# Prompt's mean squares inside the sample's projection, its norm buffers laid out first, v by head group, halo queries copied on DVE

## The chip, the cores and the metric

The kernel runs on one core of one Trainium2 chip. The metric is the device time in microseconds (us) of one execution; the time of a kernel is the median of several. The engines of a core work beside one another, each on its own instruction list in order: TensorE (PE, with its weight load PEld), VectorE (DVE), ScalarE (ACT), GpSimd (POOL) and SyncE (SP). SP and ACT also issue DMAs, each on a queue of its own; both queues end in the core's 16 DMA engines.

## The reference

One layer of a transformer trunk is applied to two sequences that share all weights: the prompt (1024 tokens) and the sample (512 tokens), each with 16 meta tokens in front, so 1040 and 528 rows of 1024 features, all in float32.

```
n    = rms_norm(x, g_mix);  proj = n @ w_in                      # 18 blocks of 128 columns
qa, ka, va (group A: 8 query heads, 2 key/value heads)           # q and k: rms_norm per head, then rope
oa   = softmax(qa ka^T * scale) va
qb, kb, vb (group B: 4 heads, each with two maps)                # rope
ob   = (softmax(q0 k0^T) - lambda * softmax(q1 k1^T)) vb;  rms_norm(ob)
x    = x + concat(oa, ob) @ w_out
n    = rms_norm(x, g_ffn)
gate = conv3(n @ w_gate) + b                                     # 3 taps along the tokens
x    = x + (gelu(gate) * (n @ w_up)) @ w_down
y    = rms_norm(x, g_final)                                      # without the 16 meta tokens
```

The convolution looks one token to either side, so of the 16 meta tokens only the last one (column 0 of the tensors `oT`) is needed behind the attention. It is got from a small extra block of queries, the halo: two columns, tokens 14 and 15, of each of the four query heads that share a key/value head.

## The kernel before

A product in float32 is made of three `fp32r` matmuls (`mm3`, L129 to L131): each operand is split into a high part (a cast on ACT, L123) and the rest (a subtraction on DVE or POOL, L124). `dense` does 8 such triples for one output tile of 128 rows by a chunk of tokens; the prompt's chunks are 384, 384 and 272 tokens wide, the sample's 256 and 272.

The work goes in five stages: (1) the sample's projection; (2) the sample's attention merged with the prompt's projection; (3) the prompt's attention merged with the sample's output projection and feed-forward part; (4) the prompt's output projection; (5) its feed-forward part. Each part is a Python generator. `merge` draws from two of them in turn by their counted cost; `LEAD1` and `LEAD2` set how far one starts ahead, and the first `HOLD` steps of the later one are held behind a mark. Within that, the framework's scheduler and its pools set the order of each engine's list. The list is then fixed: an instruction that waits holds up everything behind it on its engine. SP issues nearly all loads and stores but the weights (these go through ACT's queue, L146). Its DMAs take eight completion semaphores in turn, and each waits for the one that used the semaphore before it.

The places that the change touches:

- `projection(0)` first reads x, casts it, and adds up the squares on POOL in `acc` (L199). Then come the dense tile of the first chunk of `KA` (the keys of group A), three matmuls of `acc` with a constant matrix (`ones_d`, L208, one for each chunk) and behind each the reciprocal root on ACT and DVE (`rsqrt_newton`, L112 to L117) with `eps2` (L210), which the head norms of q and k need.
- `keys_a` (from L273) then takes each chunk through dense, a square on ACT (`sq`, L286), rope on DVE (L287, L290), `head_norm` (POOL L228, matmul L232, L112 to L117, L240) and the stores of the split result (`finish`, L247).
- Buffers come from pools that are opened and closed like a stack, from the left end of the memory for the prompt and the right for the sample. The pool `pt0` holds `sq`, `hn` and `rs_y`; it is opened behind `pb0`, which holds `y`, `z`, `hi`, `t` and `v`. A pool that is laid over a closed one takes over its waits, tile by tile: the first write to `sq` waits for the last reads of what lay there, among them a store of the sample's `y` (its pool `pb1` ended with the sample's projection).
- `attention` loads q in pairs of tiles of 512 columns (`stacked`, L370), k (L370), v (L389, `v_tail` L391), and for each head and 512 queries does four score blocks (`softmax`: matmuls L401 and L402, eviction on DVE L405 with the minimum, exponential on ACT L408). There is one score tile in PSUM, so each block waits for the eviction of the one before. The halo's queries come by 8 loads of 128 x 2 columns for each key/value head, 16 for each sequence. `reciprocals` sends a row through memory (`rT`, L458) and reads it back spread over partitions (`o_rb`, L474). The outputs go to `oT` (L563 for group B).
- Behind the sample's last head, `mixer_out` loads `h` from `oT` (L615) and residues `res` (memset L631, load L628).

## Time and profile before

| | |
|---|---|
| median of 3 runs | 2257.44 us (2257.15 to 2257.8) |
| profiled execution | 2256.74 us |
| its span | 2254.9 us |
| mean granted TensorE clock | 0.973 |
| PE busy | 2131.7 us (95%) |
| DVE, ACT, POOL busy | 1270.8, 1039.8, 666.4 us |

So 1.84 us of the profiled execution lie outside its span, and it is 0.70 us below the median. PE is busy nearly throughout and idle for 123 us in all. Below, a row of the timeline is: start, duration, engine, line, operation, output from inputs, and in square brackets how long the engine had been idle and what ended that. A row of waits is: engine and what waited, from what it waited for, total us, times, longest. A row of the chain of waits is: start, duration, what. SPq and ACTq are the queues' issuing instructions; a row with xN groups N of them.

### The profile page before, as it was taken

Reading aid. Unit: us, or ns where it says so; the run is one execution under the profiler, and the core shown is the slowest. Engines: PE = TensorE matmul, PEld = TensorE weight load, DVE = VectorE, ACT = ScalarE, POOL = GpSimd, SP = SyncE. Lnnn points to the kernel's source line nnn. Section 1 sums busy time; section 2 is a strip of 40 time slices with the busy share of each in tenths; the row PEclk is TensorE's granted clock in tenths of the full one; section 3 lists DMA queues with packets and bytes.
Section 4 is the critical chain, followed back from the end, with each engine's and each line's share of the span. In section 5 each row is a group of like instructions: output and inputs, shape, how many; then the busy total and the mean of one; then the engine's idle time right before and its main releaser. Section 6 shows DMA issues by size and latency. Waiting matters only on the chain.

```text
span 2254.9 us, 32335 instructions
## 1 busy us (share of the span) xinstructions
PE 2131.7 (95%) x12442; PEld 1912.1 (85%) x12442; DVE 1270.8 (56%) x2203; ACT 1039.8 (46%) x1830; POOL 666.4 (30%) x514
## 2 busy tenths in 40 slices
PE   6887999986799999999999997999999999999997
PEld 6886999985698888888999996998888888888887
DVE  6635554454658667667777775774433444433446
ACT  5434554655647444566777775552112221112224
POOL 5862345531023221234444443431111000111005
PEclk9998999996899999999999998999999999999999
DMA  6573453443332322232333214631111111111112
GB/s 207 177 222 110 145 162 121 158 156 113 118 101 77 94 85 84 67 94 90 115 101 107 88 66 150 191 112 53 47 38 56 47 47 48 47 38 57 47 38 76
DMA packets 114259, 222.76 MB, mean 99 GB/s; under 512 B 16312, under 2 KB 67384, under 8 KB 113592
## 3 DMA queue, kind: packets, MB, share of 16 engines
q1 hardware_dynamic: 85304, 115.82, 16.0%
q10 hardware_dynamic: 28800, 104.87, 14.6%
q8 instruction: 98, 1.61, 0.3%
q14 instruction: 57, 0.47, 0.1%
HBM read 172.10 MB, written 48.55 MB: 98 GB/s over the span
## 4 chain that ended last, share of the span: by engine, by line
PE 82%; DVE 6%; DMA 6%; ACT 3%; issue 2%; POOL 1%; SPq 1%; ACTq 0%; DVEq 0%; POOLq 0%
PE ps_mm L129 20%; PE ps_mm L130 20%; PE ps_mm L131 20%; PE ps_t L422 5%; PE ps_s L401 4%; PE ps_s L402 3%; PE ps_o L437 2%; PE ps_o L436 2%; DMA q<-qk 1%; DMA v<-v 1%; DMA w_f<-w_out 1%; DVE p L405 1%; PE ps_p L129 1%; PE ps_p L131 1%; PE ps_p L130 1%
## 5 line engine op out<-in xcount | busy, mean ns | idle before, releaser
L129 PE MATMUL ps_mm<-xhi,w_hi 128*128 128x512 f32 (+6 forms) x1968 | 663.7, 338 | 0.6 <-ACT w_hi L123 0.6
L130 PE MATMUL ps_mm<-xlo,w_hi 128*128 128x512 f32 (+6 forms) x1968 | 658.3, 335 | 0.0
L131 PE MATMUL ps_mm<-xhi,w_lo 128*128 128x512 f32 (+6 forms) x1968 | 658.2, 335 | 0.0
L129 PEld LDWEIGHTS ps_mm<-xhi,w_hi 128*128 128x128 f32 x1968 | 372.9, 190 | 27.3 <-ACT w_hi L123 0.9
L130 PEld LDWEIGHTS ps_mm<-xlo,w_hi 128*128 128x128 f32 x1968 | 373.1, 190 | 24.9 <-issue 0.5
L131 PEld LDWEIGHTS ps_mm<-xhi,w_lo 128*128 128x128 f32 x1968 | 372.8, 189 | 24.7 <-issue 0.2
L123 ACT CAST w_hi<-w_f 128x1024 fp32r<-128x1024 f32 x134 | 139.3, 1048 | 391.8 <-PE ps_mm L130 353.9
L405 DVE TENSOR_SCALAR_CACHE_REDUCE p<-ps_s 114x1044 f32<-114x1044 f32 (+5 forms) x212 | 223.5, 1054 | 138.9 <-PE ps_s L402 108.2
L124 POOL TENSOR_TENSOR a_lo<-gate,a_hi 128x512 fp32r<-128x512 f32 x66 | 98.8, 1498 | 649.2 <-ACT a_hi L123 648.2
L123 ACT CAST pt_hi<-ps_t 128x512 fp32r<-128x512 f32 (+6 forms) x360 | 169.1, 483 | 204.6 <-PE ps_t L422 174.1
L408 ACT ACTIVATE p<-p,nm 114x1040 f32<-114x1040 f32 (+5 forms) x212 | 215.1, 1015 | 86.2 <-DVE p L405 72.1
L724 DVE TENSOR_TENSOR h<-ps_mm,h 128x512 f32<-128x512 f32 (+1 forms) x288 | 182.4, 645 | 122.2 <-PE ps_mm L131 121.4
L124 DVE TENSOR_TENSOR pt_lo<-ps_t,pt_hi 128x512 fp32r<-128x512 f32 (+4 forms) x312 | 171.7, 564 | 131.9 <-ACT pt_hi L123 129.7
L401 PE MATMUL ps_s<-k,q 128*114 128x348 f32 (+4 forms) x552 | 181.3, 334 | 42.5 <-DMA q<-qk 16.9
L130 PE MATMUL ps_mm<-a_lo,w_hi 128*128 128x512 f32 (+1 forms) x576 | 216.2, 378 | 0.0
L131 PE MATMUL ps_mm<-a_hi,w_lo 128*128 128x512 f32 (+1 forms) x576 | 215.8, 378 | 0.0
L129 PE MATMUL ps_mm<-a_hi,w_hi 128*128 128x512 f32 (+1 forms) x576 | 214.9, 385 | 0.4 <-DVE h L724 0.4
L422 PE MATMUL ps_t<-ident,p 128*128 128x128 f32 (+7 forms) x1188 | 183.7, 270 | 0.4 <-DVE pt_lo L124 0.3
L402 PE MATMUL ps_s<-k,q 128*114 128x348 f32 (+4 forms) x552 | 175.4, 323 | 4.3 <-DMA q<-qk 4.3
L124 DVE TENSOR_TENSOR w_lo<-w_f,w_hi 128x1024 fp32r<-128x1024 f32 x100 | 124.1, 1250 | 83.1 <-ACT w_hi L123 82.9
L422 PEld LDWEIGHTS ps_t<-ident,p 128*128 128x128 f32 (+7 forms) x1188 | 142.7, 136 | 29.2 <-issue 4.5
L532 POOL TENSOR_TENSOR p<-p 114x1040 f32<-114x1040 f32 (+2 forms) x56 | 115.0, 2054 | 128.9 <-ACT p L531 126.9
(193 smaller groups left out, 3530.7 us busy)
## 6 DMA issues: line engine op xcount, KB each, us to landing
w_f<-w_gate ACTq DMA_DIRECT2D x44, 512.0 KB
w_f<-w_up ACTq DMA_DIRECT2D x44, 512.0 KB
w_f<-w_down ACTq DMA_DIRECT2D x44, 512.0 KB
w_f<-w_in ACTq DMA_DIRECT2D x36, 512.0 KB
w_f<-w_out ACTq DMA_DIRECT2D x32, 512.0 KB
q<-qk SPq DMA_DIRECT2D x48, 256.0 KB
q<-qk SPq DMA_DIRECT2D x48, 171.0 KB
qk<-hi SPq DMA_DIRECT2D x20, 384.0 KB
```

The costliest lines, as they stand in the source:

```text
L123: return (nc.scalar.copy(hi, src), (lo_engine or nc.vector).tensor_tensor(out=lo, in0=src, in1=hi.bitcast(F32), op=ALU.subtract))
L124: (lo_engine or nc.vector).tensor_tensor(out=lo, in0=src, in1=hi.bitcast(F32), op=ALU.subtract))
L129: nc.tensor.matmul(ps, lhsT=whi, rhs=xhi, start=start, stop=False)
L130: nc.tensor.matmul(ps, lhsT=whi, rhs=xlo, start=False, stop=False)
L131: return nc.tensor.matmul(ps, lhsT=wlo, rhs=xhi, start=False, stop=stop).ins
L401: nc.tensor.matmul(ps[:, i], lhsT=q[0], rhs=kc, start=True, stop=False)
L402: nc.tensor.matmul(ps[:, i], lhsT=q[1], rhs=kc, start=False, stop=True)
L405: nc.vector.tensor_scalar(out=p.rearrange("p (i w) -> p i w", i=nch), in0=ps, scalar1=-HD ** -0.5, scalar2=3.0e38, op0=ALU.mult, op1=ALU.m ...
L408: nc.scalar.activation(p, p, AF.Exp, bias=nm, scale=-1.0, accum_out=l)
L422: nc.tensor.transpose(tps[:, c:c + M], p[:, k0:k0 + kw], g.ident[:M, :M])
L532: nc.gpsimd.tensor_tensor(out=p0, in0=p0, in1=p1, op=ALU.add)
L724: nc.vector.tensor_tensor(out=hs, in0=ps, in1=hs, op=ALU.add)
```

## The change

Five things change at once, all before the third stage is well under way:

1. The prompt's mean squares leave the handover. The generator `projection(0)` now yields once behind them and before the load of the first weights of `KA`. The main program takes `STATS` = 26 steps of the sample's projection, then this first step of the prompt's, then the rest of the sample's.
2. For the prompt `pt0` is opened ahead of `pb0`, and stays open as long as `pb0` does.
3. `keys_a` of the prompt does the dense tile of the next chunk ahead of the rest of the chunk before, and `LEAD1` goes from -19200 to -20000.
4. v of group A lies in DRAM by key/value head (`[128, 2, tiles, 128]` in place of `[128, tiles, 256]`), so a load of v is one run of 4 KB for each of 128 partitions (before: 8 of 512 B), and its stores are two for each chunk.
5. The q tiles of the first 512 queries are 514 columns wide and start 2 columns earlier; the halo's queries are copied from them by DVE, two copies of 128 x 2 for each head, behind the eviction of the head's second block, in place of the 32 halo loads. The halo's output goes to `oT` in one store for each key/value head, before in four. The small buffers `l_b` and `r_b` have 6 copies, before 8.

```diff
@@ -176,7 +176,8 @@
             out.append(tb)
         return out
 
-    first = load_weight(g, g.w_in[KA])
+    if s == 1:
+        first = load_weight(g, g.w_in[KA])
 
     with tc.tile_pool(name=f"ps{s}", bufs=2, side=side, reuse_waits="tile") as sp:
         if s == 1:
@@ -198,8 +199,9 @@
             elif k:
                 nc.gpsimd.tensor_tensor(out=acc, in0=acc, in1=x, op=ALU.add)
         c0, cw = chunks[0]
-        first_ps = g.psum.tile(P, cw, tag)
-        dense(g, first_ps, first, xhi, xlo, c0, cw)
+        if s == 1:
+            first_ps = g.psum.tile(P, cw, tag)
+            dense(g, first_ps, first, xhi, xlo, c0, cw)
         for i, (c0, cw) in enumerate(chunks):
             if s == 1:
                 ps = ms[i]
@@ -210,9 +212,18 @@
             nc.vector.tensor_scalar(out=eps2[:, c0:c0 + cw], in0=ps, scalar1=EPS, scalar2=2 * EPS,
                                     op0=ALU.add, op1=ALU.mult)
         nc.vector.tensor_scalar(out=rstd, in0=rstd, scalar1=-0.5, scalar2=None, op0=ALU.mult)
+    if s == 0:
+        yield 0
+        first = load_weight(g, g.w_in[KA])
+        c0, cw = chunks[0]
+        first_ps = g.psum.tile(P, cw, tag)
+        dense(g, first_ps, first, xhi, xlo, c0, cw)
     es = ExitStack()
+    if s == 0:
+        tp = pool(ctx, g, f"pt{s}", 2, side)
     bp = pool(ctx, g, f"pb{s}", 2, side)
-    tp = pool(es, g, f"pt{s}", 2, side)
+    if s == 1:
+        tp = pool(es, g, f"pt{s}", 2, side)
     tab = load_tables(0)
     tab_b = load_tables(1) if s == 1 else None
     scales = {KA: [g.gain[:, V_GK:V_GK + 1], g.negain[:, V_GK:V_GK + 1]],
@@ -273,13 +284,9 @@
     def keys_a():
         cos, sin = tab
         gk, ngk = scales[KA]
-        for c0, cw in chunks:
+
+        def rest(ps, c0, cw):
             cc = slice(c0, c0 + cw)
-            if c0 == 0:
-                ps = first_ps
-            else:
-                ps = g.psum.tile(P, cw, tag)
-                dense(g, ps, first, xhi, xlo, c0, cw)
             y = tmp(bp, "y", 1, cw, 3)
             z = tmp(bp, "z", 1, cw, B1)
             sq = tmp(tp, "sq", 1, cw, 1)
@@ -291,7 +298,20 @@
                                                in1=sin[of:of + HD, cc], op0=ALU.mult, op1=ALU.mult)
             nc.gpsimd.tensor_tensor(out=y, in0=y, in1=z, op=ALU.add)
             finish(y, head_norm(sq, g.ones_hd, c0, cw, HD), g.ka[s], True, c0, cw)
+
+        late = []
+        for c0, cw in chunks:
+            if c0 == 0:
+                ps = first_ps
+            else:
+                ps = g.psum.tile(P, cw, tag)
+                dense(g, ps, first, xhi, xlo, c0, cw)
+            late.append((ps, c0, cw))
+            if s == 1 or len(late) == 2:
+                rest(*late.pop(0))
             yield 25 * cw
+        if late:
+            rest(*late.pop())
 
     def values(j):
         w = load_weight(g, g.w_in[j], lo_engine=nc.gpsimd)
@@ -321,7 +341,12 @@
                 split(g, hi, lo, pv)
                 t0 = c0 // P
                 if kw == P:
-                    nc.sync.dma_start(out=dst[:, t0 + i0:t0 + i1, :], in_=v.bitcast(F32)[:, i0:i1, :])
+                    part = v.bitcast(F32)[:, i0:i1, :]
+                    if j == VA:
+                        for m in range(2):
+                            nc.sync.dma_start(out=dst[:, m, t0 + i0:t0 + i1], in_=part[:, :, m * P:(m + 1) * P])
+                    else:
+                        nc.sync.dma_start(out=dst[:, t0 + i0:t0 + i1], in_=part)
                     continue
                 for r, part in ((16, 0), (48, 0)) if j == VA else ((16, 0), (48, 0), (80, 1)):
                     cc = slice(0, 2 * P) if j == VA else slice(part * P, (part + 1) * P)
@@ -372,7 +397,7 @@
     def load_q(j, m, c0, cw):
         out = []
         for first in range(2):
-            q = qp.tile([P, 512], F32R, name="q", tag=f"q{first}")[:, :cw]
+            q = qp.tile([P, 514], F32R, name="q", tag=f"q{first}")[:, :cw]
             stacked(q, j, m, first, c0, cw)
             out.append(q)
         return out
@@ -385,8 +410,8 @@
         return k
 
     def load_v(i, w, c0):
-        v = vp.tile([P, nf, 2 * P], F32R, name="v", tag="v")[:, :, :w]
-        nc.sync.dma_start(out=v.bitcast(F32), in_=g.v[s][i][:, :, c0:c0 + w])
+        v = vp.tile([P, nf * 2 * P], F32R, name="v", tag="v")[:, :nf * w].rearrange("p (t c) -> p t c", c=w)
+        nc.sync.dma_start(out=v.bitcast(F32), in_=g.v[s][0][:, c0 // P] if i == 0 else g.v[s][i])
         tail = vp.tile([P, P], F32R, name="v_tail", tag="v_tail")[:64 if i == 0 else 96]
         nc.sync.dma_start(out=tail.bitcast(F32), in_=g.vt[s][i][:tail.shape[0], c0:c0 + P])
         return v, tail
@@ -402,8 +427,8 @@
             nc.tensor.matmul(ps[:, i], lhsT=q[1], rhs=kc, start=False, stop=True)
 
         nm = sp.tile([P, 1], F32, name="nm", tag="nm")[:M]
-        nc.vector.tensor_scalar(out=p.rearrange("p (i w) -> p i w", i=nch), in0=ps, scalar1=-HD ** -0.5, scalar2=3.0e38,
-                                op0=ALU.mult, op1=ALU.min, accum_out=nm)
+        g.evicted = nc.vector.tensor_scalar(out=p.rearrange("p (i w) -> p i w", i=nch), in0=ps, scalar1=-HD ** -0.5,
+                                            scalar2=3.0e38, op0=ALU.mult, op1=ALU.min, accum_out=nm).ins
         p = p[:, :n]
         nc.scalar.activation(p, p, AF.Exp, bias=nm, scale=-1.0, accum_out=l)
         return p
@@ -485,15 +510,20 @@
     for kv in range(2):
         k = load_k(KA, kv)
         v = load_v(0, P, kv * P)
+        halo = [sp.tile([P, 8], F32R, name="halo", tag=f"halo{f}", bufs=2) for f in range(2)]
         for i in range(4):
             h = kv * 4 + i
             for b in range(nblk):
-                q = load_q(QA + 2 * kv, i, NMETA + 512 * b, 512)
+                q = load_q(QA + 2 * kv, i, NMETA + 512 * b - 2, 514)
                 load_r()
                 pl = []
                 l = sp.tile([P, 4], F32, name="l_a", tag="l_a", bufs=3)
                 for t in range(4):
-                    pl.append(softmax([x[:, t * P:(t + 1) * P] for x in q], k, l[:, t:t + 1]))
+                    pl.append(softmax([x[:, 2 + t * P:2 + (t + 1) * P] for x in q], k, l[:, t:t + 1]))
+                    if t == 1 and b == 0:
+                        with tc.issue_after(g.evicted):
+                            for f in range(2):
+                                nc.vector.tensor_copy(halo[f][:, 2 * i:2 * i + 2], q[f][:, 0:2])
                     yield 2 * n
                 cols = slice(1 + 512 * b, 513 + 512 * b)
                 reciprocals(l, g.rT[s][h, cols].rearrange("(t p) -> t p", p=P))
@@ -501,10 +531,6 @@
                 oa = finish_a(o, W)
                 store_a()
                 late.append((oa, g.rT[s][h:h + 1, cols], g.oT[s][h * HD:(h + 1) * HD, cols]))
-        halo = [sp.tile([P, 8], F32R, name="halo", tag=f"halo{f}", bufs=2) for f in range(2)]
-        for i in range(4):
-            for f in range(2):
-                stacked(halo[f][:, 2 * i:2 * i + 2], QA + 2 * kv, i, f, NMETA - 2, 2)
         l = sp.tile([P, 4], F32, name="l_a", tag="l_a", bufs=3)[:8, 0:1]
         load_r()
         p = softmax(halo, k, l)
@@ -513,17 +539,16 @@
         nc.scalar.activation(p, p, AF.Copy, scale=r)
         o, W = yield from weighted_v([p], v, False)
         oa = finish_a(o, W)
-        for i in range(4):
-            h = kv * 4 + i
-            nc.sync.dma_start(out=g.oT[s][h * HD:(h + 1) * HD, 0:1], in_=oa[:, 2 * i + 1:2 * i + 2])
+        nc.sync.dma_start(out=g.oT[s][kv * 4 * HD:(kv + 1) * 4 * HD, 0:1].rearrange("(i p) o -> p i o", p=HD),
+                          in_=oa.rearrange("p (i o) -> p i o", o=2)[:, :, 1:2])
         store_a()
 
     def diff_block(qs, ks, v, cols):
         pl = []
         for c0, M in cols:
-            l = sp.tile([P, 2], F32, name="l_b", tag="l_b")[:M]
+            l = sp.tile([P, 2], F32, name="l_b", tag="l_b", bufs=6)[:M]
             p0, p1 = [softmax([x[:, c0:c0 + M] for x in qs[m]], ks[m], l[:, m:m + 1]) for m in range(2)]
-            r = sp.tile([P, 2], F32, name="r_b", tag="r_b")[:M]
+            r = sp.tile([P, 2], F32, name="r_b", tag="r_b", bufs=6)[:M]
             nc.vector.reciprocal(out=r, in_=l)
             nc.scalar.activation(p0, p0, AF.Copy, scale=r[:, 0:1])
             c = sp.tile([P, 1], F32, name="c", tag="c")[:M]
@@ -803,7 +828,7 @@
 ML = 2
 NRAW, NW = 2, 3
 R1, R2 = (1.0, 1.1), (1.0, 1.0)
-LEAD1, LEAD2, HOLD = -50 * 384, 60000.0, 4
+LEAD1, LEAD2, HOLD, STATS = -20000.0, 60000.0, 4, 26
 
 
 @with_exitstack
@@ -817,7 +842,8 @@
         n = N + NMETA
         g.qk.append([dram.tile([3, 2, P, n], F32, name=f"qk{s}_{i}") for i in range(len(PAIRS))])
         g.ka.append(dram.tile([2, 2, HD, n], F32, name=f"ka{s}"))
-        g.v.append([dram.tile([P, n // P, 2 * P], F32, name=f"v{s}_{i}") for i in range(5)])
+        g.v.append([dram.tile([P, 2, n // P, P] if i == 0 else [P, n // P, 2 * P], F32, name=f"v{s}_{i}")
+                    for i in range(5)])
 
         g.vt.append(dram.tile([5, 96, 2 * P], F32, name=f"vt{s}"))
         g.oT.append(dram.tile([D, N + 1], F32, name=f"oT{s}"))
@@ -887,11 +913,15 @@
 
     g.psum = Psum(tc, "psa", mm=3)
     g.psum.relay(p=3, t=2)
-    with ExitStack() as es:
-        drain(projection(es, g, 1, "right", "p", "t"))
-    g.psum.relay(s=1, t=2, o=1)
     with ExitStack() as es0:
         p0 = projection(es0, g, 0, "left", "mm", "mm")
+        with ExitStack() as es:
+            p1 = projection(es, g, 1, "right", "p", "t")
+            for _ in range(STATS):
+                next(p1)
+            next(p0)
+            drain(p1)
+        g.psum.relay(s=1, t=2, o=1)
         with ExitStack() as es1:
             merge(g, attention(es1, g, 1, "right"), R1[0], p0, R1[1], LEAD1, HOLD)
         drain(p0)
```

In the lists of the engines, this is PE's at the handover from the first stage to the second. The matmuls with `xhi` and `xlo` are dense ones (`xhi_1674` or `xhi_1309` is the first of the eight), `acc` is the sum of squares, `sq` with `ones_hd` the head norm. Before:

```order
L130 MATMUL ps_mm<-xlo_1689,w_hi 128x384
L131 MATMUL ps_mm<-xhi_1681,w_lo 128x384
L208 MATMUL ps_mm<-acc,ones_d 128x384 x2
L208 MATMUL ps_mm<-acc,ones_d 128x272
L232 MATMUL ps_mm<-sq,ones_hd 128x384
L129 MATMUL ps_mm<-xhi_1674,w_hi 128x384
L130 MATMUL ps_mm<-xlo_1682,w_hi 128x384
```

and now:

```order
L129 MATMUL ps_mm<-xhi_1316,w_hi 128x384
L130 MATMUL ps_mm<-xlo_1324,w_hi 128x384
L131 MATMUL ps_mm<-xhi_1316,w_lo 128x384
L243 MATMUL ps_mm<-sq,ones_hd 128x384
L129 MATMUL ps_mm<-xhi_1309,w_hi 128x272
L130 MATMUL ps_mm<-xlo_1317,w_hi 128x272
L131 MATMUL ps_mm<-xhi_1309,w_lo 128x272
```

The three L208 stand no longer here (they are L210 now, one at row 538 and two at rows 658 and 659, between dense tiles of the sample's projection), the dense tile of the second chunk (rows 929 to 952) is done before the first head norm, and that of the third chunk follows it at once.

Behind these come the sample's first score blocks, each of two pairs of matmuls L401 and L402 (now L426 and L427). Before, two blocks stood behind the second dense tile and three behind the third, each time with a head norm after them, and then the first dense tile of the next weights. Now one block stands behind the third dense tile, then a head norm, three blocks, the third chunk's head norm and the next weights' first dense tile.

This is SP's list where the prompt's attention begins. `qk_0_60`, `qk_1_61` and `qk_2_62` are prompt's q and k in DRAM, `ka_66` its keys of group A, `oT_88` the sample's attention output. Before:

```order
L563 DMA oT_88<-o_b 128x207
L370 DMA q<-qk_0_60 128x1x512
L370 DMA halo<-qk_0_60 128x1x2 x8
L370 DMA k<-ka_66 128x1x1040
L370 DMA k<-ka_66 128x1x4
L389 DMA v<-v_0_67 128x8x128
L391 DMA v_tail<-vt_72 64x128
L370 DMA halo<-qk_1_61 128x1x2 x6
L563 DMA oT_88<-o_b 128x306
L370 DMA halo<-qk_1_61 128x1x2 x2
L370 DMA k<-qk_2_62 128x1x1040
L370 DMA k<-qk_2_62 128x1x4
```

and now:

```order
L395 DMA q<-qk_0_60 128x1x514 x3
L395 DMA k<-ka_66 128x1x1040
L395 DMA k<-ka_66 128x1x4
L414 DMA v<-v_0_67 128x1024
L416 DMA v_tail<-vt_72 64x128
L395 DMA k<-qk_2_62 128x1x1040
L395 DMA k<-qk_2_62 128x1x4
L395 DMA k<-qk_2_62 128x1x1040
L395 DMA k<-qk_2_62 128x1x4
L588 DMA oT_88<-o_b 128x306
L395 DMA q<-qk_0_60 128x1x514
```

The sixteen halo loads are gone, and the v load is one of 128 x 1024; the loads of k and the stores of the sample's last outputs stand directly behind one another. A few rows earlier, three of the prompt's q loads now stand ahead of a sample's q load that they stood behind or beside.

## The prediction

> **What bounds the kernel now.** I read the page first, then the waits of PE, then the chain of waits and the timeline around each long hole.
>
> ```profile
> span 2254.9 us, 32335 instructions
> ...
> PE 2131.7 (95%) x12442; PEld 1912.1 (85%) x12442; DVE 1270.8 (56%) x2203; ACT 1039.8 (46%) x1830; POOL 666.4 (30%) x514
> ...
> PE   6887999986799999999999997999999999999997
> ```
>
> PE is the bound: 123 us idle in 2254.9. A slice is 56.4 us, so the weak digits are slices 1 to 4 (up to 226 us), 9 to 11 (451 to 620) and 25. The rows below say what PE waited for.
>
> ```profile
> PE ps_s L401 <- DMA q<-qk: 16.9, 5, 5.1
> PE ps_s L401 <- DVE p L405: 13.8, 18, 4.0
> PE ps_mm L232 <- POOL sq L228: 12.5, 1, 12.5
> ...
> PE ps_s L401 <- DVE res L631: 11.4, 1, 11.4
> ```
>
> Three places carry it. The 12.5 is one hole at the handover from the sample's projection to its attention (hole 1), the 16.9 lies in the sample's last head (hole 2), the 11.4 at the start of the prompt's attention (hole 3). The chain of waits through hole 1, and ACT's timeline:
>
> ```profile
> 165.31 10.64 DMA qk<-y
> ...
> 176.59 1.00 POOL sq L228
> ```
> ```profile
> 176.02 0.49 ACT L286 ACTIVATE sq<-ps_mm 128x384 f32<-128x384 f32 x1 [9.73 <-DMA qk<-y]
> ```
>
> POOL is only the last link: ACT stood 9.73 us in front of `sq`, whose input had been ready since about 160.4, until a store of the sample's `y` had landed at 175.95, because `sq` lies where that `y` lay.
>
> **Hole 1: the norm buffers and the order of chunks.** PE's rows of the stretch, and the next weights' first dense tile in the chain:
>
> ```profile
> 160.37 1.45 PE L208 MATMUL ps_mm<-acc,ones_d 128*128 128x384 f32 x4
> 164.07 1.10 PE L208 MATMUL ps_mm<-acc,ones_d 128*128 128x272 f32 x2 [2.25 <-DVE eps L210]
> 177.63 1.65 PE L232 MATMUL ps_mm<-sq,ones_hd 128*128 128x384 f32 x2 [12.46 <-POOL sq L228]
> 186.44 0.91 PE L232 MATMUL ps_mm<-sq,ones_hd 128*128 128x384 f32 x2
> 196.41 0.59 PE L401 MATMUL ps_s<-k,q 128*128 128x264 f32 x1 [4.00 <-DVE p L405]
> ```
> ```profile
> 181.50 0.18 PE ps_mm L130
> ...
> 188.98 0.13 PE ps_mm L130
> ...
> 198.57 0.32 PE ps_mm L129
> ```
>
> From 160.37 (first dense tile done) to 198.57 are 38.2 us. With `pt0` laid out first, `sq` waits for PE alone. I walk through the new list with these rows and the following ones of ACT, DVE and POOL:
>
> ```profile
> 179.32 0.49 ACT L112 ACTIVATE rs_y<-ps_mm 128x384 f32<-128x384 f32 x1 [1.50 <-PE ps_mm L232]
> ```
> ```profile
> 181.60 0.56 DVE L115 SCALAR_TENSOR_TENSOR hn<-ps_mm,hn 128x384 f32<-128x384 f32 x1
> ...
> 185.03 0.71 DVE L405 TENSOR_SCALAR_CACHE_REDUCE p<-ps_s 128x528 f32<-128x528 f32 x1 [1.23 <-PE ps_s L402]
> 185.66 0.61 DVE L287 SCALAR_TENSOR_TENSOR y<-ps_mm,gain,rope 128x384 f32<-128x384 f32 x1
> ```
> ```profile
> 160.87 1.34 POOL L124 TENSOR_TENSOR y<-y,hi 128x544 fp32r<-128x544 f32 x1
> ```
>
> - Second dense tile, 24 x 0.18: to 164.6. Beside it ACT's square (0.49) and POOL's addition (1.00, behind the sample's last split, which ends at 162.2): ready at 163.2.
> - Head norm 0.9: 165.5. The third dense tile takes over its PSUM buffer, so it waits for three ACT steps of about 0.5, the second chunk's `sq` between them (0.5) and DVE's L115 (0.56): 2.6 us, 168.1.
> - Third dense tile, 24 x 0.13, and 1.5 for the clock (below): 172.7. First score block, four matmuls of 0.13, and a head norm: 174.1.
> - DVE from 168.1: eight steps of the head norms and rope (0.56 to 0.61) and the eviction (0.73) make 5.5, so the second block starts at 174.1, not later. The third waits for the next reciprocal root (1.6 on ACT, 0.56 on DVE) and the eviction: 177.0. The fourth: 178.5. Behind three more DVE steps that free a PSUM buffer the next dense tile starts at about 180.1.
>
> That is 19.7 us for 38.2, so 18.5 less. One score block of 0.5 is left for later, and the three mean-square matmuls are now paid at full clock among dense tiles, 1.45 + 0.5 (two thirds of a 384's 0.73). **Net -16.0.** Their roots, nineteen ACT and DVE steps of 0.5 to 0.6 or some 10 us, go beside the first stage's dense tiles. For `acc` there is room:
>
> ```profile
> 88.51 2.40 POOL L199 TENSOR_TENSOR acc<-acc,x 128x1040 f32<-128x1040 f32 x1
> ```
>
> Bounds: three q loads were issued ahead of that `y` store, so they had landed by 175.95 at the latest; if the first block gets its two no sooner, it starts 3.3 us later: -12.7. If the clock stays full and the ACT steps lie better: -18.
>
> The clock: at 164.07 the 128x272 pair took 1.10 where 0.52 is its share of the row above, after only 2.25 us of idleness; that is half speed, and I charge the third tile half of its time again. The Trainium skill, "TensorE: Matmul & The Clock Gate", "What's actually happening", has the clock halved after at least one idle window of about 3.4 us. By that a wait of 2.6 us costs no clock and the sum would be 1.5 lower. This trace's row differs, and I go by the row.
>
> **Hole 3: what SP is late with.** PE, then DVE, then SP:
>
> ```profile
> 593.32 0.66 PE L401 MATMUL ps_s<-k,q 128*128 128x348 f32 x1 [11.44 <-DVE res L631]
> ```
> ```profile
> 572.67 0.53 DVE L544 SCALAR_TENSOR_TENSOR o_b<-o_b,gsub,o_rs 128x306 f32<-128x306 f32 x1
> ...
> 579.24 0.68 DVE L124 TENSOR_TENSOR pt_hi<-ps_t,pt_hi 32x512 fp32r<-32x512 f32 x1
> ...
> 592.04 0.06 DVE L631 MEMSET res<- 128x1 f32 x1
> ```
> ```profile
> 534.37 12.21 SPq L370 DMA_DIRECT2D halo<-qk  x8
> ...
> 549.76 8.56 SPq L370 DMA_DIRECT2D halo<-qk  x6
> ...
> 558.89 1.08 SPq L370 DMA_DIRECT2D halo<-qk  x2
> ...
> 572.53 0.46 SPq L458 DMA_DIRECT2D rT<-r_rows  x1
> 580.86 0.49 SPq L474 DMA_DIRECT2D o_rb<-rT  x1
> 581.44 1.13 SPq L370 DMA_DIRECT2D q<-qk  x2
> 582.66 0.43 SPq L563 DMA_DIRECT2D oT<-o_b  x1
> ```
>
> DVE was free at 579.9 and stood until 592.0 in front of a memset of `res`, which takes the place of an `o_b` that still had to be stored. That `o_b` was done at 573.2, but its store was issued at 582.66: behind `o_rb`, which waited 8.3 us for `rT`, which SP reached late, behind 21.85 us of halo loads. It landed 9.4 us after its issue. The list has the same store behind the same `rT`, `o_rb` and q loads, without the halos. SP then reaches `rT` when its row is there (some 564), `o_rb` by 572.5 at most, and the store at about 573.3, when `o_b` is done. With 9.4 us to land: 582.7, a hole of 2.8; with half of that, none. I take **-10** (the store's 9.4 went through queues that two q loads had just filled; without the jam they drain sooner). Bounds 0 (the store waits as before) and -12.9 (the hole, and 1.5 of clock behind it as at hole 1).
>
> **Hole 2: the v load and the sample's last q.**
>
> ```profile
> 504.58 3.40 SPq L389 DMA_DIRECT2D v<-v  x1
> 508.02 6.92 SPq L391 DMA_DIRECT2D v_tail<-vt  x1
> ...
> 515.67 2.95 SPq L370 DMA_DIRECT2D q<-qk  x2
> ```
>
> The prompt's v load, 1024 runs of 512 B, held SP for 10.3 us; as 128 runs it should cost about 1, like the other loads. But the new list puts one prompt q ahead of the sample's next pair and two ahead of the pair after it, and q loads are what those PE waits end with. The bytes are the same and only their order changes, so I take **-1**, with bounds -6 (a third of the 16.9 goes) and +3 (one q load: in the 10.64 of the chain a store landed behind three of them, so some 2.7 each).
>
> **The copies.** Thirty-two DVE copies of 128x2 have no row; the nearest are
>
> ```profile
> 572.01 0.17 DVE L453 RECIPROCAL r_a<-l_a 128x4 f32<-128x4 f32 x1
> ...
> 575.70 0.07 DVE L613 MEMSET h<- 128x8 f32 x1
> ```
>
> so 32 x 0.07 to 0.17 = 2.2 to 5.4 us of DVE. A copy can delay the third block's eviction by 0.2; where dense tiles stand between the blocks PE doesn't notice. I take +1 of 0 to 5.4; without that cover it is all of it. The stores of v in twice as many pieces and the smaller `l_b`, `r_b` come at nothing: SP idles for `rT` alone 8.3 us.
>
> **Sum:** -16 - 10 - 1 + 1 = -26. From the profiled 2256.74 (span and 1.84 around it) 2230.7; its median counterpart stands 0.70 higher: **2231.4**.
>
> **The rivals.**
> - *A, hole 3 stays.* The store still follows two q loads, and `h` and `res` start as late. For: nothing shows `rT`'s 8.3 us to be due to the halos. Against: SP was busy with halos in 21.85 of the 25.6 us from 534.37. -16 - 1 + 1: 2241.4.
> - *B, hole 1 is filled by q loads or by ACT.* ACT now issues weights and a cast between the head norm's steps, and these wait for dense tiles and stores. For: the 4.00 at 196.41 is such a chain. If two thirds of hole 1 come back, -5 for -16: 2242.4.
> - *C, slower.* The first mean-square matmul sits at row 538 of PE's list, by its neighbours some 102 us in; `acc` ended at 90.9. From the point where it ends later than 102, PE stands for each us, and so do the ACT casts behind the root. To eat 26 us and more it must come at 130 or later, because its additions share POOL with the splits; with 132, 2261. Against: PE was full there, and 11 us are spare.
> - *D, it doesn't do what it says.* `pb0` now lies over the sample's buffers: if DVE's first `t` or `v` waits for the same store and that lands later than 184, hole 1 only moves; with hole 3 kept by A only the 2.25 us at 164.07 are won: 2255.2.
>
> **How the numbers follow.** Forecast 0.55, A 0.20, B 0.13, D 0.07, C 0.05. Below, all bounds good: -18 - 12.9 - 6 = -36.9, so 2220; above, A and B together give -4 to -7, so 2250. This leaves out C, D and a little. A measurement tells 0.2%, 4.5 us, from no change: faster 0.87, same 0.08, slower 0.05.
>
> **What would show it.** Right: ACT's `sq` within 1 us of the first dense tile; the next weights' dense tile at 178 to 184; no halo row on SP; the `o_b` store issued by 575 and PE's wait for `res` under 3 us. Wrong: a wait of DVE or ACT for `qk<-y` between 160 and 185; PE waiting for `q<-qk` as long as before plus what the others save; a hole before 110 us at L210.

## The result, and the profile after

| | before | changed |
|---|---|---|
| median of 4 runs each | 2257.30 us (2254.76 to 2257.80) | 2235.88 us (2229.83 to 2236.75) |
| profiled execution, its span | 2256.74, 2254.9 us | 2229.83, 2228.0 us |
| mean granted clock | 0.973 | 0.977 |

The changed kernel takes 0.9902 of the time before (95% interval 0.9882 to 0.9921): 21.4 us less by the medians, where 26 were forecast (2231.4, range 2220 to 2250). A second series gave 2233.04 us and 0.9903. The page of the changed kernel, which is of its fastest execution:

```profile
span 2228.0 us, 32312 instructions
...
PE 2131.8 (96%) x12442; PEld 1912.6 (86%) x12442; DVE 1269.7 (57%) x2235; ACT 1039.7 (47%) x1830; POOL 668.5 (30%) x514
...
PE   7898999986999999999999998999999999999997
```

PE's busy time is the same to 0.1 us, so the difference is idle time: 123.2 us before, 96.2 now. The digits of slices 3 and 4 have gone from 8 and 7 to 9 and 8, and slice 11 (564 to 620 us before) from 7 to 9; slice 10 is still 6. What PE waits for now:

```profile
PE ps_s L426 <- DMA q<-qk: 19.0, 6, 7.2
PE ps_s L426 <- DVE p L430: 12.4, 19, 2.2
...
PE ps_t L447 <- ACT r_rows L482: 2.9, 1, 2.9
...
PE ps_mm L129 <- DVE hn L115: 2.5, 1, 2.5
```

The waits for POOL's `sq` (12.5 us) and for the memset of `res` (11.4) are gone. The wait for q is not shorter but longer, 19.0 for 16.9 (with that of the second matmul of a pair, L427 and before L402, 23.9 for 21.2). ACT's timeline at the handover, then PE's:

```profile
156.37 0.49 ACT L293 ACTIVATE sq<-ps_mm 128x384 f32<-128x384 f32 x1 [1.32 <-PE ps_mm L131]
161.24 0.49 ACT L112 ACTIVATE rs_y<-ps_mm 128x384 f32<-128x384 f32 x1 [4.38 <-PE ps_mm L243]
161.63 0.48 ACT L293 ACTIVATE sq<-ps_mm 128x384 f32<-128x384 f32 x1
```
```profile
163.72 0.59 PE L129 MATMUL ps_mm<-xhi,w_hi 128*128 128x272 f32 x1 [2.52 <-DVE hn L115]
172.90 0.39 PE L426 MATMUL ps_s<-k,q 128*128 128x264 f32 x1 [2.19 <-DVE p L430]
175.58 0.59 PE L426 MATMUL ps_s<-k,q 128*128 128x264 f32 x1 [1.92 <-DVE p L430]
187.25 0.98 PE L447 MATMUL ps_t<-ident,p 128*128 128x128 f32 x4 [2.92 <-ACT r_rows L482]
```

`sq` waits for PE alone. In the handover stand three holes of 1.9 to 2.5 us in place of those of 2.25, 12.46 and 4.00; the one of 2.92 lies behind it, since the next weights' first tile starts at 177.14. SP's queue at the start of the prompt's attention:

```profile
552.52 0.27 SPq L483 DMA_DIRECT2D rT<-r_rows  x1
555.69 0.49 SPq L499 DMA_DIRECT2D o_rb<-rT  x1
...
561.53 0.34 SPq L588 DMA_DIRECT2D oT<-o_b  x1
```

`rT` takes 3.2 us until `o_rb` goes (before 8.3), and the `o_b` store goes at 561.53 (before 582.66), as soon as its `o_b` is done.

To see where the time went, I cut the execution at six places that both lists have: the prompt's first dense tile of `KA`, the first dense tile of the next weights, the first score block of the sample's last head, the 9th and the 17th score block of the prompt, and the last mean-square matmul. The times are the starts of those rows in PE's timeline; "again" is the second profile of the changed kernel, 2233.34 us.

| us | before | changed | again |
|---|---|---|---|
| start to `KA`'s first dense tile | 156.1 | 151.9 | 156.6 |
| handover, to the next weights' first tile | 41.8 | 25.2 | 25.3 |
| middle, to the sample's last head | 305.3 | 312.1 | 312.4 |
| last head, to the prompt's 9th block | 65.9 | 68.3 | 67.9 |
| prompt's blocks 9 to 16 | 47.2 | 33.7 | 33.7 |
| the rest | 1626.9 | 1625.3 | 1623.9 |

The handover gains 16.6 and the blocks 9 to 16 gain 13.5, in both profiles. The middle loses 7 and the last head 2. The rest goes from 1622.2 to 1626.9 over all the profiles, so its 1.6 and 3.0 are no more than it varies by. The start differs by 4.7 between two executions of the same kernel, so the profiled 2229.83 is lucky there.

### The profile page after: what moved, and what is told of

It reads as the page before. It is cut to its first block, busy times and chain, and to the rows that moved or that the text cites. A ratio compares the mean times of both kernels' runs of the same rounds, so it can differ in the third digit from the quotient of the medians.

```text
span 2228.0 us, 32312 instructions
## 1 busy us (share of the span) xinstructions
PE 2131.8 (96%) x12442; PEld 1912.6 (86%) x12442; DVE 1269.7 (57%) x2235; ACT 1039.7 (47%) x1830; POOL 668.5 (30%) x514
## 4 chain that ended last, share of the span: by engine, by line
PE 83%; DVE 6%; DMA 3%; ACT 3%; issue 3%; POOL 1%; SPq 1%; ACTq 0%; DVEq 0%; POOLq 0%
PE ps_mm L129 20%; PE ps_mm L130 20%; PE ps_mm L131 20%; PE ps_t L447 5%; PE ps_s L426 4%; PE ps_s L427 3%; PE ps_o L462 2%; PE ps_o L461 2%; DVE p L430 1%; PE ps_p L129 1%; PE ps_p L131 1%; PE ps_p L130 1%; DMA q<-qk 1%; PE ps_o L457 1%; PE ps_o L459 1%
## 5 line engine op out<-in xcount | busy, mean ns | idle before, releaser
L426 PE MATMUL ps_s<-k,q 128*114 128x348 f32 (+4 forms) x552 | 181.2, 333 | 31.8 <-DMA q<-qk 19.0
L427 PE MATMUL ps_s<-k,q 128*114 128x348 f32 (+4 forms) x552 | 175.0, 322 | 4.9 <-DMA q<-qk 4.9
```

Of the source, the lines that this page charges most:

```text
L426: nc.tensor.matmul(ps[:, i], lhsT=q[0], rhs=kc, start=True, stop=False)
L427: nc.tensor.matmul(ps[:, i], lhsT=q[1], rhs=kc, start=False, stop=True)
```

## The experiments

Each kernel was timed beside the kernel before. The ratios below are to that kernel in the same series; 0.001 is 2.3 us.

**The changed kernel again** (after_again). No edit.

> The changed kernel once more, for a second profile: its four runs so far go from 2229.83 to 2236.75, and the profiled one is the fastest, with the prompt's first dense tile at 151.94 us where the kernel before had it at 156.14. If the change itself shortens the first stage, that tile starts within 1 us of 152 again. If the first stage only varies from one execution to the next, it starts elsewhere between 150 and 160 and the time moves with it; the stretch from that tile to the first weights behind the keys of group A then still takes about 26 us.

2233.04 us, 0.9903 (0.9888 to 0.9918). The first dense tile starts at 156.63, so the early start of the first profile was of that execution; the handover takes 25.28 again. The first stage doesn't gain by the change; it takes in the three mean-square matmuls, 2.0 us by my estimate, without getting longer than it varies.

**Only the norm buffers first** (b_pt0), in the kernel before:

```diff
+    if s == 0:
+        tp = pool(ctx, g, f"pt{s}", 2, side)
     bp = pool(ctx, g, f"pb{s}", 2, side)
-    tp = pool(es, g, f"pt{s}", 2, side)
+    if s == 1:
+        tp = pool(es, g, f"pt{s}", 2, side)
```

> The kernel before with only the norm buffers laid out first. If the place of sq made hole 1, ACT's 9.73 us in front of sq and PE's 12.5 us for POOL's sq fall under 2 each, and the time falls by 9 to 13, to about 2246. If the rival holds that the wait only moves to DVE's first t or v, or that q loads fill the hole, it falls by less than 4.

2251.49 us, 0.9985 (0.9976 to 0.9994): 3.4 us (1.4 to 5.4). The time falls as little as the second expectation said, but not for its reason: ACT's wait is gone, as the first one said, and yet PE still stands for 5.70. ACT, then PE, of this kernel:

```profile
169.66 0.43 ACT L114 ACTIVATE rstd<-rs_y 128x272 f32<-128x272 f32 x1
170.00 0.47 ACT L289 ACTIVATE sq<-ps_mm 128x384 f32<-128x384 f32 x1
```
```profile
171.59 1.65 PE L235 MATMUL ps_mm<-sq,ones_hd 128*128 128x384 f32 x2 [5.70 <-POOL sq L231]
```

The wait for the store is gone, and `sq` now stands behind the reciprocal roots of the mean squares on ACT, which end at 170.1. The handover takes 34.9 us for 41.8. (The profiled execution, 2248.70, is one of the fastest of ten that go from 2247.65 to 2257.95, so its pieces add up to more than the 3.4.) Two causes lay one behind the other at the same place: the store until 176, the roots until 170.

**Without the norm buffers first** (a_no_pt0), in the changed kernel, the reverse of that diff:

> The changed kernel with pt0 behind pb0 again. If the place of sq is still needed beside the other parts, ACT waits for a qk<-y store in front of the first sq, PE has a hole of 6 to 10 us at the first head norm, and the time rises by 6 to 10, to about 2242. If the early mean squares and the chunk order already hide it, it rises by less than 2.

2238.44 us, 0.9921 (0.9906 to 0.9936). Its ACT and PE:

```profile
177.15 0.49 ACT L290 ACTIVATE sq<-ps_mm 128x384 f32<-128x384 f32 x1 [16.95 <-DMA qk<-y]
```
```profile
178.76 1.65 PE L240 MATMUL ps_mm<-sq,ones_hd 128*128 128x384 f32 x2 [13.04 <-POOL sq L236]
```

The hole is back in full, 13.04 us, and the handover takes 34.8 for 25.3. But by the ratios the time rises by some 4 only, less than either the hole or the first expectation, and the two intervals still overlap: the middle is 3.6 shorter than in the changed kernel, and the last head 2.1.

**With the mean squares at the handover** (a_late_stats), in the changed kernel:

```diff
-    if s == 1:
-        first = load_weight(g, g.w_in[KA])
+    first = load_weight(g, g.w_in[KA])
...
-    if s == 0:
-        yield 0
-        first = load_weight(g, g.w_in[KA])
-        c0, cw = chunks[0]
-        first_ps = g.psum.tile(P, cw, tag)
-        dense(g, first_ps, first, xhi, xlo, c0, cw)
```

(the dense tile back ahead of the mean squares for both, and the sample's projection drained before the prompt's begins).

> The changed kernel with the prompt's mean squares back at the handover. With the norm buffers alone moved (b_pt0) PE still stood 5.7 us at the first head norm, since sq came behind two of the three reciprocal roots on ACT. If that is what the early mean squares take away, a hole of 4 to 6 us returns there and the time rises by 4 to 7. If they are only moved work, the handover takes 2 us more and the first stage 2 less, and the time stays within 2.

2240.67 us, 0.9930 (0.9915 to 0.9945). PE of this kernel:

```profile
160.53 0.72 PE L208 MATMUL ps_mm<-acc,ones_d 128*128 128x272 f32 x2 [2.25 <-DVE eps L210]
163.92 0.69 PE L129 MATMUL ps_mm<-xhi,w_hi 128*128 128x384 f32 x1 [2.66 <-DVE eps L210]
```

Two holes of 2.25 and 2.66 us return, and the handover takes 29.6 us, 4.3 more, with one score block fewer in it; the time is some 6 higher. The middle, 317.9 us for 312.4, and the last head, 71.7 for 67.9, are longer too, and no run shows why. So at the handover the early mean squares count beside the place of `sq`: left out, the one costs some 6 us, the other some 4, each with an uncertainty of about 5.

**The old chunk order and lead** (a_old_keys), in the changed kernel:

```diff
-            if s == 1 or len(late) == 2:
+            if True:
...
-LEAD1, LEAD2, HOLD, STATS = -20000.0, 60000.0, 4, 26
+LEAD1, LEAD2, HOLD, STATS = -50 * 384, 60000.0, 4, 26
```

> The changed kernel with the chunks of the prompt's keys of group A in the old order (and the old lead). Each chunk's dense tile then comes behind the head norm of the one before. From the first dense tile to the next weights the changed kernel takes 25.3 us, the one before 41.8. If the chunk order carries part of that, it takes 28 to 31 and the time rises by 2 to 5; if the moved buffers and mean squares carry it all, it takes 25 to 26 and the time stays within 2.

2235.04 us, 0.9913 (0.9898 to 0.9927): within the interval of the changed kernel, so what the order is worth stays open. The handover to the next weights' first tile takes 31.9 us, but it holds one score block more and 2.8 us of waits for q, and the middle is 3.6 shorter.

**Only the halo copies** (b_halo) (with the wider q tiles, the one store and the six small buffers), in the kernel before:

```diff
+                    if t == 1 and b == 0:
+                        with tc.issue_after(g.evicted):
+                            for f in range(2):
+                                nc.vector.tensor_copy(halo[f][:, 2 * i:2 * i + 2], q[f][:, 0:2])
...
-        for i in range(4):
-            for f in range(2):
-                stacked(halo[f][:, 2 * i:2 * i + 2], QA + 2 * kv, i, f, NMETA - 2, 2)
```

> The kernel before with only the halo's queries copied on DVE (and its output in one store). If the halo loads on SP made hole 3, PE's 11.4 us for the memset of res falls under 3 and the time falls by 10 to 14, to about 2245. If the q loads ahead of the o_b store make it, the hole stays above 8 and the time falls by less than 4.

2246.64 us, 0.9964 (0.9954 to 0.9975): 8.1 us, less than the 10 to 14 of the first expectation. The blocks 9 to 16 take 31.3 us for 47.2, so hole 3 is gone. The middle takes 5.4 more and the last head 8.3 more (the profiled execution, 2252.69, is the slowest of eight, so its pieces add up to 4 only):

```profile
PE ps_s L401 <- DMA q<-qk: 22.4, 6, 10.0
```

**With the halo loads** (a_halo_loads), in the changed kernel, the reverse (its output still in one store):

> The changed kernel with the 32 halo loads again (its output still in one store). If the halos alone make the hole in front of the memset of res, it is back with 8 to 12 us, and the time rises by 9 to 14, to about 2246. If the other parts have moved SP's list far enough ahead, the hole stays under 4 and the time rises by less than 4.

2235.48 us, 0.9910 (0.9895 to 0.9925): no change that these intervals can tell from the changed kernel's 0.9902 and 0.9903. But the inside differs. Its SP and DVE:

```profile
519.54 10.06 SPq L395 DMA_DIRECT2D halo<-qk  x8
...
531.93 11.25 SPq L395 DMA_DIRECT2D halo<-qk  x8
```
```profile
571.51 0.06 DVE L655 MEMSET res<- 128x1 f32 x1 [10.22 <-DMA oT<-o_b]
```

The hole at the memset of `res` is back with 10.22 us, named this time with the store that it waits for, and the blocks 9 to 16 take 47.3 us. Against that the last head takes 61.2 us for 67.9, and the middle 309.1 for 312.4. By the time, halo loads and copies cost the same within some 5 us, at different places.

**Group A's v as before** (a_old_v), in the changed kernel:

```diff
-            nc.sync.dma_start(out=v.bitcast(F32), in_=g.v[s][0][:, c0 // P] if i == 0 else g.v[s][i])
+            nc.sync.dma_start(out=v.bitcast(F32), in_=g.v[s][i][:, :, c0:c0 + w])
```

(and its stores and the tensor in DRAM to match).

> The changed kernel with group A's v in DRAM as before (1024 runs of 512 B for a load). If the v load's descriptors hold SP and with it the sample's last q, v_tail stands some 7 us on SP again and PE's waits for q (24 us) rise by 4 to 7, the time with them. If the q loads are bound by their own four DMA engines, as a_q16 suggests, SP stands but PE doesn't notice: within 2.

2233.68 us, 0.9902 (0.9886 to 0.9919): no difference. SP stands as it did,

```profile
497.29 1.11 SPq L409 DMA_DIRECT2D v<-v  x1
498.45 7.37 SPq L411 DMA_DIRECT2D v_tail<-vt  x1
```

and PE's waits for q are 25.5 us for 23.9. With the new layout the row behind the v load takes 2.75 us of SP in place of 7.37. In the time PE doesn't notice: the last head is 2.4 shorter with it, the blocks 9 to 16 are 2.4 longer.

**The sample's q first** (a_q_first), in the changed kernel: the prompt's first q loads and its second k and v held behind the sample's last q load.

```diff
+        hold = s == 0 and (j == KA and m == 1 or j == QA and m == 0)
+        with tc.issue_after(g.last_q) if hold else nullcontext():
+            d = nc.sync.dma_start(out=tl.bitcast(F32), in_=parts[:, m, :, c0:c0 + cw])
...
```

> The changed kernel with the prompt's q loads of its first head, and its second k and v, held on SP behind the sample's last q load; nothing else. Without the halo copies (a_halo_loads) the sample's last q stood ahead of the prompt's and PE's waits there were some 8 us shorter. If that order is the whole of it, PE's waits for q fall from 24 to some 14 us, the hole at res stays away, and the time falls by 7 to 11 against the changed kernel. If four DMA engines work off the same bytes whatever their order, the prompt's first score blocks wait by as much as the sample's last ones gain, and the time stays within 3.

2234.44 us, 0.9908 (0.9894 to 0.9923): no change, and the second expectation holds, though one wait later than it said. The waits for q and PE behind them:

```profile
PE ps_s L431 <- DMA q<-qk: 12.9, 6, 4.5
```
```profile
573.71 0.42 PE L431 MATMUL ps_s<-k,q 128*128 128x348 f32 x1 [3.21 <-DVE res L661]
```

The waits fall by 6, and the last head takes 63.3 us for 67.9; then a wait for `res` of 3.21 is back, and the blocks 9 to 16 take 38.3 for 33.7. Order alone only moves the loss.

**q and k loads over sixteen DMA engines** (a_q16), in the changed kernel. The rows of a score's contraction may stand in any partition if q and k agree, so the view of the source can be turned:

```diff
-        parts = src[first:first + 2].rearrange("p x (m r) n -> (p x) m r n", r=32)
-        nc.sync.dma_start(out=tl.bitcast(F32), in_=parts[:, m, :, c0:c0 + cw])
+        parts = src[first:first + 2].rearrange("p x (m r) n -> m r (p x) n", r=32)
+        nc.sync.dma_start(out=tl.bitcast(F32), in_=parts[m, :, :, c0:c0 + cw])
```

> The changed kernel with other rows in the partitions of the q and k tiles (row r of part x in partition 4r+x, not 32x+r, the same in q and k, so the scores are the same): the slowest dimension of a load is then 32, not 4. The DMA share was 22 to 26% while only q loads ran. If that is four of sixteen DMA engines and this is what the sample's last head waits for, the loads spread over sixteen, PE's waits for q (24 us in the changed kernel) fall under 8 and the time falls by 12 to 20. If SP's order or the release of the q tiles makes these waits, they stay above 18 and the time stays within 4.

2205.72 us, 0.9777 (0.9757 to 0.9797): 49 us below before, 27 to 30 below the changed kernel, more than expected. All that is left of the waits for q:

```profile
PE ps_s L426 <- DMA q<-qk: 2.0, 1, 2.0
```

The last head takes 49.3 us for 67.9, and the middle 301.6 for 312.4. How busy the DMA engines are around the same four k loads of the prompt, while no other queue moves anything, in the changed kernel (531 to 539 us) and with the turned view (504 to 508); the columns are packets, MB and share of 16 engines:

```profile
q1 hardware_dynamic: 353, 0.81, 25.7%
```
```profile
q1 hardware_dynamic: 545, 1.22, 94.0%
```

That is 101 GB/s for 305. A share of 25.7% is what 4.1 of the 16 engines would make if they were always busy, which is an estimate from this row. The Trainium skill, "DMA: Bandwidth & Descriptors", "Why a DMA increments its semaphore by 16 and not by 1", has such a DMA run on the largest number up to 16 that divides the slowest dimension of both sides. By that the old view, [4, 32, width] against 128 partitions, runs on 4 engines and the turned one, [32, 4, width], on 16. The shares above agree with that. What the run shows is that turning the view alone does it, and that the share rises 3.7 times; the number of engines itself is in no row, and the turned view also reads DRAM in another order, which no run separates from it.

**The same in the kernel before** (b_q16), the same diff:

> The kernel before with the q and k loads spread over sixteen DMA engines. If only the waits for q go (21 us, and some slow clock), the time falls by 20 to 28, and holes 1 and 3 stay at 10 us and more each. If the store in front of sq, the halos and the o_b store were late through the same four engines, holes 1 and 3 shrink too and the time falls by 35 or more; the change would then be worth under 15 on top of it.

2210.48 us, 0.9808 (0.9792 to 0.9825): 45 us, the second expectation. Two lines take away twice what the whole change does. The stretch from 165 to 176 us, with its share of DMA time and GB/s in the last two columns, before and with the turned view:

```profile
165.00:176.00 11.00, 0.17 (x1) 0.00 (x0) 1.55 (x3) 1.22 (x3) 0.00 (x0) 0.50 0.32 119
```
```profile
165.00:176.00 11.00, 4.70 (x12) 3.59 (x13) 5.87 (x12) 4.90 (x10) 0.99 (x1) 0.54 0.61 182
```

and SP of this kernel where the prompt's attention begins, with all 32 halo loads:

```profile
505.10 5.13 SPq L370 DMA_DIRECT2D halo<-qk  x8
...
512.92 4.13 SPq L370 DMA_DIRECT2D halo<-qk  x6
...
517.74 1.16 SPq L370 DMA_DIRECT2D halo<-qk  x2
...
532.64 0.27 SPq L458 DMA_DIRECT2D rT<-r_rows  x1
533.83 0.48 SPq L474 DMA_DIRECT2D o_rb<-rT  x1
```

The prompt's sixteen halo loads take 10.4 us of SP (before 21.85), `rT` 1.2 us until `o_rb` goes (before 8.3), and the blocks 9 to 16 take 33.7 us, as in the changed kernel: hole 3 is gone with the halo loads in place. At the handover `sq` comes at 170.44 for 176.02, still behind a wait of 2.97 us on ACT for a DMA, and PE's hole is 6.05 for 12.46; the handover takes 35.1 us, as with the norm buffers alone. On top of the turned view the change is worth 5 us by the medians (a_q16), where it was worth 21.

**Both, with the halo loads** (a_halo_q16): the changed kernel with the turned view and the halo loads again.

> a_q16 with the 32 halo loads again. If each halo load keeps SP for as long with the q loads spread over sixteen DMA engines (22 us for the prompt's sixteen), the o_b store is late again, a hole of 8 to 12 us stands at the memset of res, and the time is 8 to 12 above a_q16's 2205.7. If it is the jam behind the q loads that makes them slow, they take about 0.5 us each, some 8 in all, the hole stays under 3 and the time within 3.

2197.52 us, 0.9744 (0.9730 to 0.9759), the fastest of all: 60 us under the kernel before by the first series' median, 58 by its own, and 13 under b_q16. It is 8.2 us faster than with the copies (7.4 by the ratios), which neither expectation held possible. The middle takes 296.2 us for 301.6, the blocks 9 to 16 take 35.5 for 33.7, and the first dense tile came 3.0 earlier, which is within what the start varies by. Part 5 makes the middle longer in all three pairs of kernels with and without it (by 5.4, 3.3 and 5.3 us). Why, I didn't find, and its copies were not tried apart from its wider q tiles that start 2 columns earlier: PE idles 1.9 us of the 100 from 306 us on with the copies and 0.3 without, and the rest lies in another order of the two parts' work.

## Why the prediction came out right, point by point

The time lies in the range, 4.5 us above the forecast. The waits of holes 1 and 3 are gone by the mechanisms named, but that the sum comes so close is luck: errors cancel in it. Split with the help of a_halo_loads, the second profile is 23.5 us shorter up to the last cut: some 12 are hole 1 (forecast 16), 3.7 are hole 3 and the copies together (forecast 9), 4.7 lie in the last head without the copies (forecast 1), where no run separates the cause, and 3.0 lie in the rest, for which the sum has no term. Each of these is a difference of single profiles, good to a few us. In the order of its steps, with the numbers of the second profile, the more usual one:

- *Hole 1, -16.0.* The mechanism is right: the place of `sq` made the hole (b_pt0, a_no_pt0), and the early mean squares count beside it (a_late_stats). What the chunk order adds stays open (a_old_keys). The walk through the new list said 18.5 less to the next weights' tile; it is 16.6. Of the 1.9, 0.6 lies in the base: the prediction took the tile's start before from the chain's row, 198.57, where PE's timeline has it at 197.98. The third dense tile waits 2.52 us for `hn` (2.6 said), and q was there but for 0.38. The walk holds to within 0.6 us up to the third score block; the fourth came 1.3 later than said. What failed is the step that set the net at 18.5 less 0.5 and 2.0. The middle is 7.1 us longer, of which I had only the score block of 0.5. With the halo loads (a_halo_loads) it is 3.8 longer, so 3.3 of the 7.1 come with part 5. With the other 3.8 and the start's 0.5, hole 1 gave about 12 us net, not 16. The sums of the windows over the middle, of the kernel before and of the second profile, give PE's busy time:
```profile
sum 305.28, PE 300.01 PEld 284.20 DVE 157.15 ACT 161.57 POOL 133.64; mean PE 60.00 PEld 56.84 DVE 31.43 ACT 32.31 POOL 26.73
```
```profile
sum 312.42, PE 301.43 PEld 284.17 DVE 162.02 ACT 164.00 POOL 134.76; mean PE 60.28 PEld 56.83 DVE 32.40 ACT 32.80 POOL 26.95
```

  PE idles 11.0 us in it for 5.3, with 1.4 more of work and slow clock. Of the 5.7, 3.1 are a wait that I hadn't named: PE for `r_rows`, the row of reciprocals at the end of the sample's first group of queries (2.92 in the first profile, quoted above); another 1.5 are waits for q. ACT is late with `r_rows` because of the cast ahead of it in its list, in the first profile

```profile
186.62 0.42 ACT L123 CAST hi<-y 128x272 fp32r<-128x272 f32 x1 [6.77 <-DMA ka<-hi]
186.94 0.25 ACT L482 COPY r_rows<-ps_t 4x128 f32<-4x128 f32 x1
```

  which waits until the keys' first store has left one of the two `hi` buffers. That store is issued 14.7 us earlier than before (172.74 for 187.48), but it keeps SP for 4.55 us (before 0.42), and its buffer is free only at 186.6.
- *The clock.* Behind 2.52 us of idleness the third dense tile ran at half speed for 3.1 us, as charged (first profile):
```profile
164.34 0.43 PE L131 MATMUL ps_mm<-xhi,w_lo 128*128 128x272 f32 x1
164.57 0.43 PE L129 MATMUL ps_mm<-xhi,w_hi 128*128 128x272 f32 x1
...
167.27 0.29 PE L130 MATMUL ps_mm<-xlo,w_hi 128*128 128x272 f32 x1
167.40 0.29 PE L131 MATMUL ps_mm<-xhi,w_lo 128*128 128x272 f32 x1
```

  The starts are 0.23 us apart up to 166.84 and then 0.13; the granted clock is 0.50 in the first stretch and 0.99 behind it. The Trainium skill's rule ("TensorE: Matmul & The Clock Gate", "What's actually happening"), half clock after an idle window of about 3.4 us, doesn't cover this hole, or that of 2.25 before; the trace goes on differing from it there.
- *Hole 3, -10.* It gave 13.5, a little over the bound of 12.9. The chain is as described: with the halos gone SP came to the store at 561.5, and nothing was late there. But the reason stops one step short: halos are slow and `rT` is late because q and k loads stand ahead of them that keep only a quarter of the DMA engines' time busy; with these turned, the hole is gone and the halo loads stay (b_q16). The rival A, that the hole stays, is out.
- *Hole 2, -1.* With the copies the last head cost 2.0, within the bounds. The v load cost PE nothing (a_old_v). The v load should have held SP for about 1 us and held it for 4.0 (1.28 and the 2.75 behind it, for 10.3). That the prompt's q loads in front eat the gain was right, but another order only moves the loss on to the blocks 9 to 16 (a_q_first).
- *The copies, +1.* The copies themselves took 5.6 us of DVE in the first profile, 0.23 for a pair but for two pairs of 1.1 and 1.2; the bound was 5.4. Their effect on the time can't be told apart. With the halo loads the changed kernel is as fast within some 5 us, and with the q loads spread it is 8 us faster; so no gain of part 5 shows here, where the prediction had it carry 9 of 26, and b_halo's 8.1 don't add to the rest. Its gain at hole 3 is given back in the middle and in the last head, by a_halo_loads' pieces 13.7 against 3.3 and 6.7.

The rival C has no support: the first stage has no hole at L210. Of B a small part came true: a cast on ACT waits for a store, but behind the handover, and it costs PE 3.1 us, not two thirds of hole 1. Of D nothing showed: no wait of DVE or ACT for a `qk<-y` store is left at the handover.

## What to carry to other kernels

Before moving loads around a wait, look at how busy they keep the DMA engines: a stretch in which only they run and the DMA share stays near a quarter (25.7% here) was the sign, and the order of dimensions in the access pattern the cure (94.0%), free wherever the rows may be permuted. Parts tried alone and parts left out don't add up (halo copies: 8.1 us alone, 0 to 2 left out): a hole that closes at one place lets the next queue run into the same jam, so cut the profile at places that both lists have, and sum the pieces before crediting a part.

## What the hardware showed that I had not expected

A load of 8-byte runs isn't as slow in itself as it looked. The same sixteen halo loads took 21.85 us of SP among q and k loads in the old view, and 10.4 us among the turned ones, 0.65 each for 1.37. And the first stage, nearly the same code in all kernels, took from 151.9 to 158.5 us in the profiles, a spread of 6.5 us, nearly that of the four runs of the changed kernel (6.9).
